# Strassen–Winograd products in 19 of 22 gate and up pairs instead of 12, with the weight sums begun from the first head

## The chip, the cores and the metric

The kernel runs on one core of a Trainium2 chip. The metric is the device time of one execution in microseconds; several executions were timed, and their median counts. The core has a TensorE (PE) that multiplies, with a loader for its weights (PEld), a VectorE (DVE), a ScalarE (ACT), a GpSimd (POOL) and a SyncE (SP), which run their own instruction streams in order. DMA transfers are issued from the streams of SP, ACT and POOL; in the profile SP's transfers are queue q1 and POOL's queue q0.

## The reference, cut to what matters

One residual block on 512 tokens of width 1024: two token mixers side by side (a gated delta rule with 8 heads, and a convolution of 31 taps), a projection, then a SwiGLU channel mixer of hidden width 2816, then a norm. All in float32.

```python
h = rmsnorm(x, norm1_w[l])
proj = h @ w_in[l]
...                                   # 8 heads of the gated delta rule -> out_a; convolution -> out_b
...                                   # gates, w_out and the residual give x; then the channel mixer:
h = rmsnorm(x, norm2_w[l])
gate, up = jnp.split(h @ ffn_w_gate_up[l], 2, axis=-1)
x = x + (jax.nn.silu(gate) * up) @ ffn_w_down[l]
...
return rmsnorm(x, norm_f_w)
```

2816 hidden columns are 22 tiles of 128. For each there is a gate tile and an up tile, 1024 x 128 weights each; this is a "pair" below.

## The kernel before, in words

Every float32 product is made of three: an operand is split into a rounded high part and the rest (`whi`, `wlo` for weights, `hh`, `hl` for the normed tokens), and `split3` issues high by high, high by low and low by high. All weights come through `unit()`: a load of up to 512 KB into `raw` on SP's queue, a copy to `whi` on ACT (L111), a subtraction to `wlo` on DVE (L112). Buffers rotate in a pool, and a load waits only for its buffer.

The program has three stages. **Phase 1** (the page's 0 to about 420 us) walks over 8 heads. A queue of generators yields one set of products after another, and `count` counts its steps; conv, decay and solve work of the heads is hung between them, so each engine's stream mixes several heads. Of a head's work POOL does a power of the key norms (`ss`, L464), a scaling (`Un`, L474), small copies (`cp`, `cc`, L481 to L486), then a solve of 15 dependent steps (`ytm`, `y`, L502 and L504, which need `U`, brought by eight DMAs), and the masks of the decays (`DT`, L444). ACT takes `DT` at L449, the scaled keys at L512 (`Vp`), the solution `y` at L557. **The middle** (to about 603 us) is the output projections, gates and the second norm. **The channel mixer** computes gate and up, 22 pairs, then the down product, itself in Strassen–Winograd form.

A gate and up pair can be computed in two ways. The plain way (`for f in range(F0)`) is 2 weight tiles by 8 contraction tiles by 3 products = 48 products of 512 columns. The other, `pair(f)`, takes gate and up as the two rows, the contraction halves and the token halves as the rest of a 2 by 2 by 2 block product, and needs 7 block products for 8: 7 x 4 x 3 = 84 products of 256 columns. It needs sums of token blocks (`T1` to `T4`, made once by the list `todo`, each item a DVE or ACT step over 128x1024) and four sums of weight blocks for every pair, `s1` to `s4`, 256 KB each. After its 84 products DVE combines the blocks (`cu`, `cv`, `cw`, `fm`).

The sums of weights are made in DRAM, without an engine: `feed_one()` takes the next item of the list `feed`, copies one weight block to the sum's tile (SP's queue, L192), and two items later POOL issues a DMA that adds the other block onto it (L196). `s2` adds `s1`, and `s4` adds `s2`, so these wait for the sum before. In phase 1 nothing is fed until `count` reaches 335; from there `fill()`, called in every `unit()`, feeds one item in two of three calls, later in each, and also makes sums of the down weights on POOL (`dsums_add`, L172, `wst`, `wsh`). `issue_after` sets an instruction behind another in its engine's stream; a scheduler sets the rest.

`pair(f)` uses four PSUM banks for its block results, from two pools: `bank()` is one of the five of `psw`, `bank2()` one of the three of `psm`. Even and odd pairs take four and one of the five. The down product that follows takes four banks of `psw` (`p1`, `p5`).

Of the kernel before, what the change touches and what calls it, by code (L numbers as in the profile page):

```python
# [20 lines left out]
FF = 22  # L21
# [11 lines left out]
def block_kernel(ctx, tc, a):  # L33
# [51 lines left out]
    def marked(b, kind="drain"):  # L85
        mark[b.ins.engine, kind] = b.ins
        return b

    @contextmanager
    def behind(only=None):  # L90
        with ExitStack() as st:
            for i in list(mark.values()):
                if only is None or i.engine == only:
                    st.enter_context(tc.issue_after(i))
            yield

    loads, start_feed, gps_ = [], [False], []

    last = [None]

    def unit(ap, pool=None):

        aps = ap if isinstance(ap, tuple) else (ap,)
        n = T * len(aps) if isinstance(ap, tuple) else 1024
        raw, hi, lo = ((pool or wp).tile([P, n if pool else 1024], t, name=x)[:, 0:n]
                       for t, x in ((F32, "raw"), (F32R, "whi"), (F32R, "wlo")))
        for i, p in enumerate(aps):
            loads.append(nc.sync.dma_start(raw[:, i * T:(i + 1) * T] if len(aps) > 1 else raw, p))
        if start_feed[0]:
            fill()  # L110
        marked(S.activation(hi, raw, AF.Copy), "unit")  # L111
        marked(V.tensor_tensor(out=lo, in0=raw, in1=hi.bitcast(F32), op=ALU.subtract), "unit")  # L112
        return hi, lo
# [31 lines left out]

    FK, F0 = FF // 2, 10
    sums = {n: dram.tile([FF - F0, P, T], F32, name=n, bufs=1) for n in ("s1", "s2", "s3", "s4")}
    gu = {n: a["wgu"][r * FF + F0:(r + 1) * FF][:, :, c * T:(c + 1) * T]  # L150
          for n, r, c in (("A11", 0, 0), ("A12", 0, 1), ("A21", 1, 0), ("A22", 1, 1))}
# [16 lines left out]
    def dsums_add(k, r, cs=slice(0, T)):  # L168
        b11, b12, b21, b22 = (r[:, i, :] for i in range(4))
        with tc.issue_after(last[0].ins):  # L170
            for o, x, y in ((b22, b12, b22), (b12, b11, b12), (b11, b22, b11), (b21, b11, b21)):
                G.tensor_tensor(out=o, in0=x, in1=y, op=ALU.add)  # L172
        nc.gpsimd.dma_start(wsum[k][:, :, cs], r)

    def half_load():
        k, cs = halves.pop(0)
        if len(gps_) == 1:
            r = gps_[0].tile([P, 16, NT, 16], F32, name="U", bufs=2)
            r = r.rearrange("p k n c -> p (k n c)").rearrange("p (i c) -> p i c", i=4)
        else:  # L180
            r = gps_[1].tile([P, 4, 256], F32, name="wsh", bufs=1)
        with tc.issue_after(loads[-1].ins):
            dsums_load(k, r, nc.sync, cs)
        taken.append((k, r, cs))

    def feed_one(n=1):

        for _ in range(n):
            if feed:
                w, p, m, other = feed.pop(0)  # L190
                with tc.issue_after(loads[-1].ins):
                    nc.sync.dma_start(sums[w][p], gu[m][p])  # L192
                begun.append((sums[w][p], other[p]))
        while len(begun) > (2 if feed else 0):
            with tc.issue_after((fed[-1] if fed else last[0]).ins):
                fed.append(nc.gpsimd.dma_start(*begun.pop(0), accum_op=ALU.add, max_dma_last_dim=2048))  # L196
# [3 lines left out]
    def fill():  # L200

        units[0] += 1
        if units[0] % 3 != 2 or not gps_:
            feed_one()
        if taken and units[0] % 3 != 2 and not norming[0]:
            dsums_add(*taken.pop(0))
        if halves and gps_ and units[0] > 3 and not taken and not norming[0] and (units[0] % 2 == 0 if len(gps_) == 1 else units[0] % 3 == 0):
            half_load()
# [528 lines left out]
    def step():  # L737

        while queue:
            try:  # L740
                next(queue[0])
            except StopIteration:
                queue.pop(0)
                continue
            count[0] += 1
            if count[0] % 8 == 0:
                background()
            return True
        return False
# [15 lines left out]
    def background():  # L765
        prio = tc.cur_priority
        tc.cur_priority = prio + OFF
        while len(convs) < len(cs):
            conv31(len(convs), cs[len(convs)])
            convs.append(1)  # L770
        tc.cur_priority = prio
# [63 lines left out]
    done, ended, dts, convs, count, chains = [], [], [], [], [0], [[0, decays()]]  # L835
# [4 lines left out]
    queue.append(rest)  # L840
    nh = 0
    while step() or chains:
        start_feed[0] = count[0] >= 335
        if nh < H and count[0] >= START - 9 + 32 * nh + sum(OTHERS[:nh]):
            chains.append([0, chain(*done[nh])])
            nh += 1
        for c in list(chains):
            if c[0] <= count[0] or not queue:
                with behind():
                    n = next(c[1], None)  # L850
                if n is None:
                    chains.remove(c)
                else:
                    c[0] = count[0] + n
    background()
    for _, sc, e in ended:
        if not sc:
# [170 lines left out]
    def hidden():  # L1028
        fms.append(fp.tile([P, T], F32, name="fm"))
        return fms[-1]  # L1030
# [38 lines left out]
    def negated():  # L1069
# [4 lines left out]
    todo = [joined(b11, kl, t1), joined(b12, kl, t2), lambda: tt(b11, b11, b12, ALU.subtract),  # L1074
            joined(b22, kh, t2), lambda: tt(b12, b22, b12, ALU.subtract),
            lambda: tt(b22, b22, b11, ALU.add), joined(b21, kh, t1),
            lambda: tt(b21, b22, b21, ALU.subtract),
            lambda: xsplit(*T4, b21), negated, lambda: xsplit(*T3, b12)]
# [3 lines left out]
    def some_operands(f):  # L1082
        if not ff:
            fxs.close()
            ff.append(ctx.enter_context(tc.tile_pool(name="ff", bufs=FK)))
        for _ in range(3 if f < F0 else 2):
            if len(made) <= f:
                operands(len(made))
                made.append(1)

    def next_todo():
        if todo:
            with behind():
                todo.pop(0)()

    for f in range(F0):
        start_feed[0] = f > 0
        dsums_to(f)
        if f > 1:
            pg = psm.tile([P, T], F32, name="mm")  # L1100
            col_tile(pg, a["wgu"][f], hhk, hlk)
        else:
            pg = first[2 * f][0]
            k_loop(*first[2 * f], slice(2 * P, T))
        sg = fq.tile([P, T], F32, name="cw", bufs=2)
        S.activation(sg, pg, AF.Silu)
        if f:
            next_todo()
            pu = psm.tile([P, T], F32, name="mm")
            col_tile(pu, a["wgu"][FF + f], hhk, hlk)  # L1110
        else:
            pu = first[1][0]
            k_loop(*first[1], slice(2 * P, T))
        tt(hidden(), pu, sg, ALU.mult)
        if f:
            next_todo()
        if f > 6:
            some_operands(f)

    def hprod(ps, w, i, x):  # L1120

# [4 lines left out]
    bank = lambda: psw.tile([P, T], F32, name="w")  # L1126
    bank2 = lambda: psm.tile([P, T], F32, name="mm")

    def pair(f):

        z = [bank() for _ in range(4)] if f % 2 == 0 else [bank(), bank2(), bank2(), bank2()]
        s = lambda n: sums[n][f - F0]
        w = unit(a["wgu"][f])
        w46 = unit((a["wgu"][FF + f][:, T:], s("s2")))
        hprod(z[0][:, t1], w, 0, B11)
        hprod(z[1][:, t1], w, 1, B21)
        hprod(z[2][:, t1], w46, 0, T4)
        w37 = unit((s("s4"), s("s3")))
        hprod(z[0][:, t2], w46, 1, T2)
        cw = fq.tile([P, T], F32, name="cw", bufs=2)  # L1140
        S.copy(out=cw[:, t1], in_=z[0][:, t1])
        u = fq.tile([P, TH], F32, name="cu")
        tt(u, cw[:, t1], z[0][:, t2], ALU.add)
        hprod(z[1][:, t2], w37, 0, B22)
        w5 = unit((s("s1"),))
        hprod(z[3][:, t1], w37, 1, T3)
        v = fq.tile([P, TH], F32, name="cv2")
        tt(v, u, z[3][:, t1], ALU.add)
        if f == F0:
            xsplit(*T1, b11)  # L1150
        hprod(z[2][:, t2], w5, 0, T1)
        tt(cw[:, t2], u, z[2][:, t2], ALU.add)
        fm = hidden()
        tt(fm.rearrange("p (i t) -> p i t", i=2), z[2].rearrange("p (i t) -> p i t", i=2),
           v.rearrange("p (a t) -> p a t", a=1).broadcast_to([P, 2, TH]), ALU.add)
        tt(cw, cw, z[1], ALU.add)
        S.activation(cw, cw, AF.Silu)
        V.scalar_tensor_tensor(out=fm, in0=fm, scalar=-1.0, in1=cw, op0=ALU.mult, op1=ALU.mult)
# [230 lines left out]
```

## Time and profile before

| | |
|---|---|
| time, median of 3 runs (lowest to highest) | 941.8 us (941.11 to 942.73) |
| the profiled execution | 943.44 us, span 941.7 us |
| granted TensorE clock | 0.997 |
| busy share of the span | PE 98%, PEld 83%, DVE 79%, ACT 59%, POOL 36% |
| q1 (SP's transfers) | 144.89 MB, 44.9% of the 16 DMA engines' span |
| q0 (POOL's transfers) | 28.90 MB, 13.3% |
| accumulating transfers (L196) | 48, 256 KB each |

A row of the chain of waits has a start, a length and what filled it. A group's row has its busy time, the mean in ns, and after a second bar the idle time of its engine just before it, with what ended it. A row of the timeline has start, length, engine, line and operation; the bracket is the idle time before it and what released it.

### The profile page before, as it was taken

What the parts mean: (1) busy time and instruction counts of PE and PEld (TensorE: products, weight loads), DVE (VectorE), ACT (ScalarE), POOL (GpSimd) and SP (SyncE); (2) the same over time, 40 slices, a digit from 0 to 9 for tenths busy, and PEclk for the clock granted to TensorE, in tenths of its full rate; (3) what the DMA queues carried; (4) which work ended last, traced back from release to release, by engine and by line L of the source; (5) the groups of instructions that cost most, each with busy time, mean ns of one, the idle gap of its engine ahead of it and who ended that gap; (6) DMA issues with size and microseconds to landing.
All of it is one profiled execution on the core that took longest, in us unless ns stands there. A gap on an engine that the chain in (4) does not pass through costs nothing.

```text
span 941.7 us, 14545 instructions
## 1 busy us (share of the span) xinstructions
PE 925.4 (98%) x4952; PEld 785.3 (83%) x4952; DVE 740.8 (79%) x1157; ACT 558.0 (59%) x1278; POOL 336.8 (36%) x541
## 2 busy tenths in 40 slices
PE   9999999999999999999999999999999999999996
PEld 6777788878888888888888888988889999988885
DVE  4889898989989899999587643676536877888896
ACT  6696977888778796643555323324324445466545
POOL 0134345253353437544055341245531111133042
PEclk9999999999999999999999999999999999999999
DMA  9333413223123246989898983699797564577654
GB/s 322 113 114 118 131 68 103 86 85 108 73 77 103 93 136 159 335 263 268 284 286 279 285 236 127 205 292 288 257 257 213 184 197 168 186 236 255 213 181 148
DMA packets 78187, 177.39 MB, mean 188 GB/s; under 512 B 10080, under 2 KB 19472, under 8 KB 77088
## 3 DMA queue, kind: packets, MB, share of 16 engines
q1 hardware_dynamic: 66528, 144.89, 44.9%
q0 software_dynamic: 10288, 28.90, 13.3%
q10 hardware_dynamic: 1296, 2.67, 0.7%
q8 instruction: 39, 0.64, 0.3%
q14 instruction: 36, 0.29, 0.1%
HBM read 156.22 MB, written 45.37 MB: 214 GB/s over the span
## 4 chain that ended last, share of the span: by engine, by line
PE 82%; ACT 7%; DVE 3%; issue 1%; POOL 1%; DMA 1%; POOLq 0%; ACTq 0%; DVEq 0%; SPq 0%
PE mm L121 55%; PE w L121 20%; PE b L526 2%; DVE wlo L112 1%; ACT whi L111 1%; PE g L435 1%; PE g L470 1%; PE st L639 1%; PE st L630 1%; PE st L638 1%; PE st L624 1%; PE st L625 0%; ACT Un L473 0%; DVE xs L964 0%; PE b L435 0%
## 5 line engine op out<-in xcount | busy, mean ns | idle before, releaser
L111 ACT ACTIVATE whi<-raw 128x1024 fp32r<-128x1024 f32 (+1 forms) x191 | 196.4, 1030 | 242.6 <-PE mm L121 158.0
L112 DVE TENSOR_TENSOR wlo<-raw,whi 128x1024 fp32r<-128x1024 f32 (+1 forms) x191 | 239.6, 1256 | 86.1 <-ACT whi L111 84.8
L121 PE MATMUL mm<-hh,whi 128*128 128x512 f32 (+1 forms) x688 | 269.7, 392 | 1.2 <-ACT whi L111 0.8
L121 PE MATMUL mm<-hh,wlo 128*128 128x512 f32 (+1 forms) x688 | 264.2, 385 | 0.8 <-DVE wlo L112 0.8
L121 PE MATMUL mm<-hl,whi 128*128 128x512 f32 (+1 forms) x688 | 263.0, 382 | 0.0
L693 DVE SCALAR_TENSOR_TENSOR cps<-c,c31w,cps 128x512 f32<-128x512 f32 x224 | 167.9, 749 | 3.8
L121 PEld LDWEIGHTS mm<-hh,wlo 128*128 128x128 f32 x688 | 130.0, 189 | 25.0 <-DVE wlo L112 1.3
L121 PEld LDWEIGHTS mm<-hh,whi 128*128 128x128 f32 x688 | 130.3, 189 | 22.9 <-ACT whi L111 1.7
L121 PEld LDWEIGHTS mm<-hl,whi 128*128 128x128 f32 x688 | 130.3, 189 | 20.9
L1022 POOL TENSOR_TENSOR fm<-fm 128x256 f32<-128x256 f32 x33 | 28.1, 852 | 117.7 <-DVE s L1022 93.2
L422 DVE SCALAR_TENSOR_TENSOR acc<-mm,c4w,acc 128x511 f32<-128x511 f32 (+2 forms) x72 | 53.0, 740 | 4.3 <-ACT acc L419 4.1
L502 POOL TENSOR_TENSOR ytm<-U,y 128x60 f32<-128x60 f32 (+14 forms) x120 | 36.7, 306 | 51.0 <-DMA U<-sc 42.2
L121 PE MATMUL mm<-yh,whi 128*128 128x512 f32 x128 | 50.6, 396 | 0.0
L121 PE MATMUL mm<-yh,wlo 128*128 128x512 f32 x128 | 49.8, 389 | 0.0
L121 PE MATMUL mm<-yl,whi 128*128 128x512 f32 x128 | 49.8, 389 | 0.0
L121 PE MATMUL w<-hh,wlo 128*128 128x256 f32 x168 | 47.7, 284 | 0.3 <-DVE wlo L112 0.3
L121 PE MATMUL w<-hh,whi 128*128 128x256 f32 x168 | 47.6, 284 | 0.0
L121 PE MATMUL w<-hl,whi 128*128 128x256 f32 x168 | 47.5, 283 | 0.0
L196 POOL DMA_DIRECT2D s<-in_wgu_dram x24 | 22.7, 962 | 64.0 <-DMA s<-in_wgu_dram 64.0
L121 PE MATMUL w<-wlo,fh 128*128 128x512 f32 (+1 forms) x115 | 44.3, 385 | 0.2 <-DVE wlo L112 0.2
L121 PE MATMUL w<-whi,fl 128*128 128x512 f32 (+1 forms) x115 | 44.2, 385 | 0.0
L121 PE MATMUL w<-whi,fh 128*128 128x512 f32 (+1 forms) x115 | 44.2, 385 | 0.0
(346 smaller groups left out, 1937.5 us busy)
## 6 DMA issues: line engine op xcount, KB each, us to landing
raw<-in_win_dram SPq DMA_DIRECT2D x61, 512.0 KB, 3.2
raw<-in_wgu_dram SPq DMA_DIRECT2D x32, 512.0 KB, 3.2
s<-in_wgu_dram SPq DMA_DIRECT2D x48, 256.0 KB, 5.3
raw<-s SPq DMA_DIRECT2D x48, 256.0 KB, 3.6
raw<-wsum SPq DMA_DIRECT2D x44, 256.0 KB, 3.6
raw<-in_wdn_dram SPq DMA_DIRECT2D x33, 256.0 KB, 3.2
s<-in_wgu_dram POOLq DMA_DIRECT2D x24, 256.0 KB, 6.8
s<-s POOLq DMA_DIRECT2D x24, 256.0 KB, 7.2
```

Source lines behind the costliest of these rows:

```text
L111: marked(S.activation(hi, raw, AF.Copy), "unit")
L112: marked(V.tensor_tensor(out=lo, in0=raw, in1=hi.bitcast(F32), op=ALU.subtract), "unit")
L121: marked(PE.matmul(ps, l, r, start=first and i == 0, stop=last and i == 2))
L196: fed.append(nc.gpsimd.dma_start(*begun.pop(0), accum_op=ALU.add, max_dma_last_dim=2048))
L422: marked(V.scalar_tensor_tensor(out=acc[:, s:], in0=ps[:, :T - s], scalar=c4w[:, j, k:k + 1], in1=acc[:, s:], op0=ALU.mult, op1=ALU.add))
L435: PE.transpose(ps[:, n, :], src[:, n, :], ident)
L470: PE.matmul(ps[:, n, :], kT[:, n, :], kT[:, n, :], start=True, stop=True)
L502: G.tensor_tensor(out=tm[:, :, 0:w], in0=U[:, k, :, k + 1:], in1=y[:, :, k:k + 1].broadcast_to([P, NT, w]), op=ALU.mult)
L526: PE.matmul(ps[:, q, 0:w], stationary[:, q, :], moving[:, q, :], start=True, stop=True)
L624: PE.matmul(ps[:, 0, :], kT[:, n, :], Sp, start=True, stop=True)
L693: V.scalar_tensor_tensor(out=acc if k < 30 else cv[i], in0=c[:, k:k + T], scalar=c31w[:, i, k:k + 1], in1=acc if k > 1 else cv[i], op0=ALU ...
L1022: return eng.tensor_tensor(out=out, in0=in0, in1=in1, op=op)
```

## The change

`F0` goes from 10 to 3, so pairs 3 to 21 (19) use 7 block products and pairs 0 to 2 the plain way; the list `feed` grows from 48 to 76 items. A flag `ahead` is set from step 64 of phase 1: every `unit()` then feeds one item, until `fill()` takes over at step 335 as before. The items of `todo` are done two at a time, in the three plain pairs and in the first calls of `pair`. The late operands of the down product (`some_operands`) come only from the loop over pairs, two per call. The choice of the PSUM banks counts from `F0`, so the last pair (21) now takes four of `psw`, where it took one.

```diff
+        elif ahead[0]:
+            feed_one()
...
-    FK, F0 = FF // 2, 10
+    FK, F0 = FF // 2, 3
...
     while step() or chains:
+        ahead[0] = count[0] >= 64
         start_feed[0] = count[0] >= 335
...
+    ahead[0] = False
...
-        for _ in range(3 if f < F0 else 2):
+        for _ in range(2):
...
     def next_todo():
-        if todo:
+        for _ in todo[:2]:
             with behind():
                 todo.pop(0)()
...
-        if f:
-            next_todo()
-        if f > 6:
-            some_operands(f)
+        next_todo()
...
     def pair(f):
-        z = [bank() for _ in range(4)] if f % 2 == 0 else [bank(), bank2(), bank2(), bank2()]
+        z = [bank() for _ in range(4)] if (f - F0) % 2 == 0 else [bank(), bank2(), bank2(), bank2()]
         s = lambda n: sums[n][f - F0]
         w = unit(a["wgu"][f])
+        next_todo()
```

Lines behind the second edit stand two lower in the changed kernel (L196 is L198, L464 is L466). Three places in the streams show what moves. The first is POOL in phase 1, between the end of head 1's solve (`y`) and the start of head 2's. Before:

```order
L504 TENSOR_TENSOR y_1056<-y_1056,ytm_1100 128x4 [waits Pool_49]
L464 TENSOR_TENSOR ss_1452<-ss_1452,root4_85 128x4 [waits DVE_49]
L474 TENSOR_TENSOR Un_1476<-Un_1476,DT_991 128x512 [waits Activation_49]
L481 COPY cp_1482<-Un_1476 32x128 [waits Pool_49]
L481 COPY cp_1482<-Un_1476 32x128 x3
L484 TENSOR_SCALAR cc_1483<-cp_1482,cst_76 128x64 [waits Pool_49]
```

The same place in the changed kernel:

```order
L506 TENSOR_TENSOR y_1056<-y_1056,ytm_1100 128x4 [waits Pool_49]
L198 DMA s1_125<-in_wgu_dram 128x512
L198 DMA s3_127<-in_wgu_dram 128x512
L198 DMA s2_126<-s1_125 128x512 [waits DMASW2_49]
L198 DMA s1_125<-in_wgu_dram 128x512
L198 DMA s4_128<-s2_126 128x512 [waits DMASW4_49]
L466 TENSOR_TENSOR ss_1460<-ss_1460,root4_85 128x4 [waits DVE_49]
L198 DMA s3_127<-in_wgu_dram 128x512
L198 DMA s2_126<-s1_125 128x512 [waits DMASW5_49,DMASW0_49]
L198 DMA s1_125<-in_wgu_dram 128x512 [waits DMAHW2_49,DMASW1_49]
L476 TENSOR_TENSOR Un_1484<-Un_1484,DT_991 128x512 [waits Activation_49]
```

Five accumulating DMAs stand ahead of the norms' power (`ss`), eight ahead of `Un`, and two of the five wait for the accumulate before them to land.

The second is SP behind the second norm's store (`ysp`), where the channel mixer's loads are issued. Before:

```order
L962 DMA ysp<-A 128x1024
L192 DMA s_126<-in_wgu_dram 128x512
L108 DMA raw<-in_wgu_dram 128x1024
L192 DMA s_125<-in_wgu_dram 128x512
L108 DMA raw<-in_wgu_dram 128x1024
L192 DMA s_128<-in_wgu_dram 128x512
L108 DMA raw<-in_wgu_dram 128x1024
```

After, from the fourth unit behind the store on:

```order
L194 DMA s_126<-in_wgu_dram 128x512
L108 DMA raw<-in_wgu_dram 128x512
L108 DMA raw<-s_126 128x512
L194 DMA s_125<-in_wgu_dram 128x512
L108 DMA raw<-s_128 128x512
L108 DMA raw<-s_127 128x512
L194 DMA s_128<-in_wgu_dram 128x512
L108 DMA raw<-s_125 128x512
L194 DMA s_127<-in_wgu_dram 128x512
L108 DMA raw<-in_wgu_dram 128x1024
```

In both a copy follows every unit. Before, 20 copies follow the store and lie beside plain pairs, two units to a pair; now 17 do, and 13 of them lie beside pairs 3 to 6, four units to a pair.

The third is PE at the end of the last pair, where the down product begins. Before:

```order
L121 MATMUL mm_8747<-hh_92,wlo_8835 128x256
L121 MATMUL w_8889<-whi_8894,fh_7101 128x512 [waits Activation_49]
L121 MATMUL w_8889<-whi_8894,fl_7102 128x512
L121 MATMUL w_8889<-wlo_8895,fh_7101 128x512 [waits DVE_49]
L121 MATMUL w_8890<-whi_8894,fh_7101 128x512
L121 MATMUL w_8890<-whi_8894,fl_7102 128x512
L121 MATMUL w_8890<-wlo_8895,fh_7101 128x512
L121 MATMUL w_8891<-whi_8894,fh_7101 128x512 [waits PE_49]
```

After:

```order
L123 MATMUL w_9223<-hh_92,wlo_9311 128x256
L123 MATMUL w_9365<-whi_9370,fh_6939 128x512 [waits Activation_49]
L123 MATMUL w_9365<-whi_9370,fl_6940 128x512
L123 MATMUL w_9365<-wlo_9371,fh_6939 128x512 [waits DVE_49]
L123 MATMUL w_9366<-whi_9370,fh_6939 128x512 [waits DVE_49]
L123 MATMUL w_9366<-whi_9370,fl_6940 128x512
L123 MATMUL w_9366<-wlo_9371,fh_6939 128x512
L123 MATMUL w_9367<-whi_9370,fh_6939 128x512 [waits DVE_49]
```

The second and third banks (`w_9366`, `w_9367`) are ones that the last pair's combination on DVE still reads.

More of the change, by code (lines that the diff above doesn't have):

```diff
@@ L95, in behind @@
             yield
[L97 removed]
+    loads, start_feed, ahead, gps_ = [], [False], [False], []
     last = [None]
```

## The prediction

> **What bounds the kernel now.** I read first the page's engine shares, then the windows by stage, then the chain of waits, then PE's waits, and last the streams of the engines that the change loads. The windows (PE, PEld, DVE, ACT, POOL busy, granted clock, DMA share, GB/s):
>
> ```profile
> 60.00:420.00 360.00, 354.02 (x1860) 293.27 (x1859) 327.14 (x613) 279.07 (x856) 165.29 (x359) 1.00 0.39 125
> 616.00:708.00 92.00, 92.00 (x408) 76.20 (x407) 51.94 (x44) 28.90 (x40) 43.04 (x40) 1.00 0.90 278
> 646.00:656.00 10.00, 10.00 (x46) 8.29 (x45) 4.59 (x5) 4.51 (x5) 1.71 (x3) 1.00 1.00 312
> 708.00:829.00 121.00, 121.00 (x1009) 120.98 (x1009) 92.92 (x139) 59.47 (x84) 16.98 (x22) 1.00 0.60 190
> 740.00:750.00 10.00, 10.00 (x86) 10.00 (x85) 7.94 (x13) 5.01 (x7) 1.54 (x2) 1.00 0.58 185
> ```
>
> PE is busy without a gap where gate and up are computed, in the plain pairs (616 to 708) and the 7-product pairs (708 to 829) alike. So a product less there is time less, as long as nothing else comes late. The chain of waits, in order of time, gives the price of both kinds:
>
> ```profile
> 615.49 92.51 PE mm L121 x408
> 708.00 11.51 PE w L121 x96
> 719.51 2.88 PE mm L121 x24
> 722.39 1.44 PE w L121 x12
> 723.83 4.32 PE mm L121 x36
> 728.15 11.52 PE w L121 x96
> ...
> 808.79 11.52 PE w L121 x96
> 820.31 2.88 PE mm L121 x24
> ```
>
> 408 products of 512 columns took 92.51 us, 0.2268 each; a plain pair is 48, 10.886 us. From 708.00 to 728.15 two 7-product pairs run: 96 + 24 + 12 + 36 = 168 products of 256 columns in 20.15 us, 0.1199 each; a pair is 84, 10.08 us. The gain is 0.81 us a pair, 7.4% and not an eighth, since half the columns cost 53% of the time.
>
> **The products.** Seven pairs (3 to 9) change kind: 7 x 0.81 = **-5.64 us**. The three plain pairs left stay as they are.
>
> **The bank at the end.** The last pair now takes four `psw` banks, so the down product's third bank is the one `cw` reads last. DVE's rows there before:
>
> ```profile
> 829.71 0.41 DVE L1022 TENSOR_TENSOR cw<-cu,mm 128x256 f32<-128x256 f32 x1
> 830.04 0.68 DVE L1022 TENSOR_TENSOR fm<-mm,cv 128x512 f32<-128x512 f32 x1
> 830.64 0.68 DVE L1022 TENSOR_TENSOR cw<-cw,mm 128x512 f32<-128x512 f32 x1
> 828.78 0.40 PE L121 MATMUL w<-whi,fh 128*128 128x512 f32 x1
> ```
>
> The down product begins at 828.78, wants its third bank six products later, 828.78 + 6 x 0.2268 = 830.14, and the last reader ends at 831.32. PE is in order, so it stands for **+1.2 us**. Ends: 0, if DVE's `cw` comes ahead of `fm` there; 2.4, if the subtraction for the next weights, which stands behind these three, is then late too. I take 1.2, which two rows of this place give.
>
> **Phase 1.** 28 more copies and 28 more accumulates; all items ahead of step 335 are new there, so POOL's part is not 28 but about 35 instructions between the heads. One accumulate's price, and how long until the next may follow:
>
> ```profile
> L196 POOL DMA_DIRECT2D s<-in_wgu_dram x24 | 22.7, 962 | 64.0 <-DMA s<-in_wgu_dram 64.0
> L196 POOL DMA_DIRECT2D s<-s x24 | 21.6, 901 | 42.0 <-DMA s<-s 28.2 <-DMA s<-in_wgu_dram 13.7 <-issue 0.2
> 366.85 0.81 POOL L196 DMA_DIRECT2D s<-s  x1 [0.62 <-DMA s<-in_wgu_dram]
> 372.55 0.81 POOL L196 DMA_DIRECT2D s<-s  x1 [1.09 <-DMA s<-s]
> ```
>
> About 0.9 us of POOL each, some 32 us over phase 1, in which POOL is busy 165 of 360. Dearer is the wait: 372.55 - 366.85 = 5.7 us from one accumulate to the one that needs it. Head 2 is the worst place:
>
> ```profile
> 133.79 1.03 POOL L464 TENSOR_TENSOR ss<-ss,root 128x4 f32<-128x4 f32 x1 [8.47 <-DVE ss L462]
> 141.45 0.35 ACT L512 ACTIVATE Vp<-g,ss 128x128 f32<-128x128 f32 x1
> 160.11 0.21 POOL L504 TENSOR_TENSOR y<-y,ytm 128x4 f32<-128x4 f32 x1
> 161.28 1.29 POOL L444 TENSOR_TENSOR DT<-DT,cst 128x512 f32<-128x512 f32 x1
> 162.61 0.40 ACT L449 ACTIVATE DT<-DT,sm 128x128 f32<-128x128 f32 x1 [2.95 <-POOL DT L444]
> 184.43 0.34 ACT L557 ACTIVATE YY<-y,cst 128x64 f32<-128x64 f32 x1
> ```
>
> POOL is free from 125.32 (133.79 - 8.47). Five accumulates with two waits: 125.32 + 2 x 5.7 + 0.8 = 137.5, so `ss` ends near 138.5, 3.7 us later than its 134.8, and ACT wants it at 141.45: hidden. Six more stand ahead of the solve; with 0.9 each and a wait or two I put the end of `y` about 10 us later, near 170, against ACT's `YY` at 184.43: hidden. Then `DT` comes near 174 instead of 162.6. ACT's stream has also moved there: its `DT` step now stands behind a weight copy, the key's activation and three more steps, about 168.5 by the lengths of those in the trace; ACT waits some 5.5 us where it waited 2.95. Behind it in ACT's stream stand the reads of PSUM for the next convolutions; a bank of PE is 24 products x 0.2268 = 5.4 us, so PE has one bank's cover, and ACT idles 29.7 us for PE in this stretch, in which it can catch up:
>
> ```profile
> ACT whi L111 <- PE mm L121: 29.7, 15, 4.1
> ```
>
> I take **+0.7 us**. Ends: -1 (PE's few microseconds of waits in phase 1 fall otherwise in the new order) and +6 (two such waits, each a few microseconds past the cover). The copies on SP's queue are 28 x 256 KB over some 260 us at a DMA share of 0.39; the raw loads there have time in hand, so nothing for them.
>
> **Transfers beside pairs 3 to 6.** This is the disputed term. Before, the copies lay beside plain pairs; their load was 0.90 of the engines over 92 us and PE never stood, not even at 1.00 (646 to 656). Now 13 copies lie beside four pairs, one a unit. A pair's loads are 3 x 512 + 256 KB = 1.84 MB, its copies 1.05 MB: 2.9 MB in 10.08 us on q1, 286 GB/s; the `wst` loads of 1 MB and their stores, one of each in two pairs, add 100 GB/s on q0, a third of that, without the accumulates. The windows have 278 to 312 GB/s at 0.90 to 1.00. So for pairs 3 to 6 the demand is some 20% above what those windows moved: over 30 us about 6 us of transfers fall behind. What a pair has in hand, and the transfers' sizes and landings:
>
> ```profile
> 817.39 1.06 ACT L111 ACTIVATE whi<-raw 128x1024 fp32r<-128x1024 f32 x1 [1.56 <-PE w L121]
> 818.83 1.06 ACT L111 ACTIVATE whi<-raw 128x1024 fp32r<-128x1024 f32 x1 [0.38 <-PE w L121]
> 818.49 1.23 DVE L112 TENSOR_TENSOR wlo<-raw,whi 128x1024 fp32r<-128x1024 f32 x1 [0.60 <-ACT whi L111]
> raw<-in_wgu_dram SPq DMA_DIRECT2D x32, 512.0 KB, 3.2
> s<-in_wgu_dram SPq DMA_DIRECT2D x48, 256.0 KB, 5.3
> wst<-in_wdn_dram POOLq DMA_DIRECT2D x4, 1024.0 KB, 8.1
> ```
>
> ACT's copies wait for PE to free a buffer, not for the load. The `wlo` of 818.49 ends at 819.72, and PE needs that unit 36 products into the pair that starts at 818.87 (808.79 + 84 x 0.12): counted with the first product of its high part, 24 after, 821.75. So 2.0 us in hand behind ACT and DVE, and about 1 us ahead of them, since a load must also wait for its buffer: landings may grow from 3.2 to about 6 us before PE stands. Of 6 us behind, some 3 to 4 are covered, and 2 would reach PE. I take **+1.5 us**: ends 0 (646 to 656, no PE wait at full load) and +6 (all the backlog).
>
> **POOL's additions beside DVE.** Three of the four `wst` bursts now lie beside 7-product pairs, where DVE is busy 7.94 of 10 us:
>
> ```profile
> 655.74 6.62 POOL L172 TENSOR_TENSOR wst<-wst 128x512 f32<-128x512 f32 x4 [6.05 <-DMA wst<-in_wdn_dram]
> 617.94 2.31 DVE L112 TENSOR_TENSOR wlo<-raw,whi 128x1024 fp32r<-128x1024 f32 x1
> 643.62 1.23 DVE L112 TENSOR_TENSOR wlo<-raw,whi 128x1024 fp32r<-128x1024 f32 x1
> ```
>
> A subtraction takes 2.31 us beside an addition and 1.23 alone. Such two-input steps are about 0.6 of DVE's work in a pair, so in 6.62 us of additions DVE falls 5.3 x 1.53 - 6.62 = 1.5 us behind; there are 2.0 us in hand: **+0.3 us** for the three, from 0 to 3.
>
> The Trainium skill (SBUF — State Buffer, "Who interferes with whom") says that a DVE step with two SBUF inputs and a GpSimd step that reads SBUF exclude each other for the whole instruction. The 2.31 against 1.23 agrees with a wait, of 1.08 us and not of an addition's whole 1.66 (6.62 / 4); by the rule at its worst the term would be the port rival's below.
>
> **The rest.** `todo` has the same 11 steps, now two at a time: by their lengths (1.22 us each) the operands are ready near 630, before pair 3 begins at 615.49 + 72 x 0.2268 = 631.8 us; nothing, though the margin is 1 to 2 us. The late operands are spread one or two per pair; ACT is busy 5.01 of 10 us. The 59 sums fed before the channel mixer are early for pair 3. Nothing each.
>
> Sum: -5.64 + 1.2 + 0.7 + 1.5 + 0.3 = -1.9 to -2.3 (the margins overlap, so I round to **-2.2**). The profiled execution took 943.44 us, span 941.7, 1.6 above the median of 941.8; the sum against it gives 941.2, against the median **939.6 us**.
>
> **The rivals.**
> (a) All is hidden but the bank, or not even that: -5.64 + 0 to 1.2, 936.2 to 938. For it: PE did not stand at DMA share 1.00. Against it: the doubled units per time.
> (b) The transfers eat the gain: the term is 4 to 6 instead of 1.5, 941 to 943.7. For it: copies and raw loads share one queue, in order, so each load stands behind a 256 KB copy that took 5.3 us at the median. The Trainium skill (DMA: Bandwidth & Descriptors, "Queues, rings and completion order") has the engines take turns between queues packet by packet, which would give POOL's transfers an equal turn against the loads while both have work; no row of before splits the two, and the rule speaks for this rival.
> (c) Slower: POOL's stream in phase 1. If accumulates land in 8 us rather than 5.7, beside 15 dependent steps, `DT` comes at 180, not 174, ACT stands for some 11 us and PE runs out of free banks after 5.4: +6 at each of the two late `DT`, so -5.64 + 1.5 + 2 x 5 = +6: 945 to 949. It decides from an ACT wait of about 5.4 us on. Against it: 24 us in hand at `YY`, and only those places.
> (d) The port: each of three `wlo` in a burst waits out a whole addition of 1.66 us (6.62 / 4), 5 us late, 3 past what is in hand, in two or three bursts: -5.64 + 1.2 + 0.7 + 6 to 9, 944 to 947. For it: DVE is busier there than before. Against it: 2.31 us, not 2.9, is the longest `wlo` of before.
>
> **How the numbers follow.** This kernel's runs spread by 0.17%, so a change of under 0.2% (1.9 us) counts as none; faster means below 939.9, slower above 943.7. Forecast, 938.3 to 941.0: 0.42, of which 0.26 below 939.9. (a) 0.18, faster. (b) 0.22, within. (c) 0.12 and (d) 0.06, slower. Faster 0.44, same 0.38, slower 0.18. The range, 936.8 to 945.3, leaves out the lower third of (a) and most of (c), and the forecast's own range is the one named above.
>
> **What would show it.** Right: PE rows of 7-product pairs from 631.8 on in the chain at 10.08 us each; a gap of about 1.2 us on PE behind six down products, ended by DVE; PE waits of 1 to 2 us on `whi` or `wlo` in the first four such pairs, none later; `DT` on ACT waiting 4 to 6 us near 170 with PE's phase 1 ending within 1 us of before. Wrong: the output projections' start later by over 3 us, for (c); over 3 us of waits in pairs 3 to 6 ended by a DMA, for (b), or by `wlo` during `wst`, for (d); none of all these, for (a).

## The result: slower, and the profile after

The changed kernel takes 965.55 us (median of 4 runs, 964.2 to 965.84) against 942.1 before (median of 4); the ratio is 1.0247, interval 1.0229 to 1.0265. The profiled run took 964.2 us with a span of 962.4, so 20.7 us more than the span before. The chain of waits divides it. These are its rows at the start of the channel mixer, at pair 3, where the first unbroken 7-product pair comes back, and at the last pair (start, length, what):

```profile
612.02 11.52 PE w L123 x96
623.54 16.35 PE mm L123 x72
639.88 10.09 PE w L123 x84
...
719.32 11.52 PE w L123 x96
...
840.28 40.82 PE w L123 x219
```

The row of 96 small products that opens the channel mixer stood at 603.97 before and is at 612.02 now: **8.05 us are lost ahead of the channel mixer**. That is one execution's figure: in five experiments below whose phase 1 is edited no further, the row stands 4.6 to 9.75 us late, so it moves by several microseconds. The three plain pairs take what they took (72 products in 16.35). Pair 3 begins at 639.88, right behind them. The pairs from 719.32 on run without a wait, two in 20.16 us, to the last at 840.28; 719.32 is then pair 9, and pairs 3 to 8 took 79.44 us instead of 6 x 10.08 = 60.48: **19.0 us are lost there**. From the last row, 40.82 - 84 x 0.12 = 30.74 us go to the down product's first 135 products, against 30.63 before. With the products' -5.64 and -0.7 behind the pairs, 8.05 + 19.0 - 5.64 - 0.7 = 20.7.

The windows of phase 1 where it is lost, and of pairs 3 to 8 (PE, PEld, DVE, ACT, POOL busy, granted clock, DMA share, GB/s). The first row is the kernel before, the others are the changed kernel:

```profile
140.00:200.00 60.00, 59.49 (x324) 49.02 (x323) 52.97 (x107) 51.59 (x164) 26.36 (x64) 1.00 0.27 90
140.00:200.00 60.00, 54.16 (x272) 44.74 (x271) 45.06 (x92) 40.45 (x135) 34.84 (x64) 0.91 0.71 164
144.00:146.00 2.00, 2.00 (x7) 1.51 (x6) 1.26 (x2) 1.94 (x7) 1.89 (x3) 0.50 1.12 199
182.00:184.00 2.00, 0.00 (x0) 0.00 (x0) 2.00 (x5) 2.00 (x7) 1.35 (x1) 1.00 0.00 0
186.00:188.00 2.00, 1.76 (x8) 1.76 (x9) 1.93 (x4) 1.96 (x10) 1.91 (x2) 0.50 0.77 256
188.00:190.00 2.00, 2.00 (x10) 2.00 (x10) 1.34 (x4) 1.92 (x7) 1.73 (x5) 0.50 0.53 201
640.00:708.00 68.00, 58.40 (x443) 56.42 (x442) 40.57 (x53) 23.57 (x34) 31.52 (x28) 0.94 0.97 304
711.00:714.00 3.00, 3.00 (x16) 3.00 (x16) 2.26 (x4) 2.10 (x3) 0.81 (x1) 0.50 0.76 195
```

Two things are to be seen. In 140 to 200 and in 640 to 708 PE is idle for 5.8 and 9.6 us. And behind the idle stretches the granted clock is 0.50 for some microseconds, though PE is busy again: 144 to 146, 186 to 190, 711 to 714. The loss is idle time and half speed together; the busy time hides the second part. Of the 79.4 us of pairs 3 to 8 PE is idle for 11.4, at a mean clock of 0.91; the other 7.6 us of the 19.0 are mostly slower running. At 140 the changed kernel was ahead (ACT's `Un` of head 2 at 133.86 against 135.67 before), so 140 to 200 lost somewhat more than the 8.05. In 640 to 708 the transfers are at 0.97 of the 16 engines for 68 us.

Who waited in phase 1, by the streams of POOL, ACT, DVE and PE:

```profile
127.33 1.85 POOL L198 DMA_DIRECT2D s<-in_wgu_dram  x2
133.60 0.81 POOL L198 DMA_DIRECT2D s<-s  x1 [4.43 <-DMA s<-in_wgu_dram]
139.26 0.81 POOL L198 DMA_DIRECT2D s<-s  x1 [4.01 <-DMA s<-s]
139.81 1.33 POOL L466 TENSOR_TENSOR ss<-ss,root 128x4 f32<-128x4 f32 x1
141.17 0.37 ACT L514 ACTIVATE Vp<-g,ss 128x128 f32<-128x128 f32 x1 [1.44 <-POOL ss L466]
142.48 0.49 PE L640 MATMUL st<-w,kd 128*128 128x128 f32 x2 [1.54 <-ACT R L637]
172.39 0.21 POOL L506 TENSOR_TENSOR y<-y,ytm 128x4 f32<-128x4 f32 x1
173.95 1.92 POOL L446 TENSOR_TENSOR DT<-DT,cst 128x512 f32<-128x512 f32 x1
175.90 1.28 ACT L451 ACTIVATE DT<-DT,sm 128x128 f32<-128x128 f32 x4 [4.26 <-POOL DT L446]
180.43 0.75 DVE L424 SCALAR_TENSOR_TENSOR acc<-mm,c4w,acc 128x511 f32<-128x511 f32 x1 [4.98 <-ACT acc L421]
184.56 0.47 PE L123 MATMUL mm<-hh,whi 128*128 128x512 f32 x1 [3.07 <-DVE ss L468]
```

The bracket at the end of each row is the wait. POOL waits 4.43 and 4.01 us for one accumulate and then the next, so `ss`, `y` and `DT` of head 2 come late. Behind `ss` ACT waits 1.44 us and PE 1.54. Behind `DT` ACT waits 4.26 us, DVE 4.98 for ACT's copy of a convolution, and PE 3.07 for DVE. The profile names DVE's small step `ss` as the releaser of PE; that PE waits for a PSUM bank is an inference, from DVE's reading of a bank (`acc<-mm`, L424) up to 184.42, just ahead of PE's 184.56.

Who waited beside the pairs, 636 to 722 us, from the waits view (total, times, longest):

```profile
ACT whi L113 <- DMA raw<-s: 32.2, 13, 7.7
DVE wlo L114 <- ACT whi L113: 29.2, 14, 6.9
PE mm L123 <- ACT whi L113: 4.8, 1, 4.8
PE w L123 <- DVE wlo L114: 3.0, 5, 0.9
```

The weights land late, and ACT, DVE and PE wait behind one another.

### The profile page after: what moved, and what is told of

Read it like the earlier page. It is cut to its first block, busy times and chain, and to the rows that moved or that the text cites. A ratio compares the mean times of both kernels' runs of the same rounds, so it can differ in the third digit from the quotient of the medians.

```text
span 962.4 us, 15283 instructions
## 1 busy us (share of the span) xinstructions
PE 930.9 (97%) x5204; PEld 800.3 (83%) x5204; DVE 761.7 (79%) x1206; ACT 568.6 (59%) x1297; POOL 367.0 (38%) x569
## 4 chain that ended last, share of the span: by engine, by line
PE 68%; DMA 8%; ACT 6%; DVE 6%; POOL 4%; issue 2%; SPq 1%; POOLq 0%; ACTq 0%; DVEq 0%
PE mm L123 40%; PE w L123 22%; DMA raw<-s 4%; DVE wlo L114 2%; PE b L528 1%; DMA U<-sc 1%; POOL ytm L504 1%; ACT whi L113 1%; DVE cps L695 1%; POOL y L506 1%; PE st L641 1%; DMA s<-in_wgu_dram 1%; PE g L437 1%; POOL s L198 1%; DMA s<-s 1%
## 5 line engine op out<-in xcount | busy, mean ns | idle before, releaser
L123 PE MATMUL mm<-hh,whi 128*128 128x512 f32 (+1 forms) x612 | 236.3, 387 | 4.2 <-DVE ss L468 3.1
L123 PE MATMUL mm<-hh,wlo 128*128 128x512 f32 (+1 forms) x612 | 231.4, 378 | 0.2 <-DVE wlo L114 0.2
L123 PE MATMUL mm<-hl,whi 128*128 128x512 f32 (+1 forms) x612 | 230.2, 376 | 0.0
L123 PE MATMUL w<-hh,wlo 128*128 128x256 f32 x244 | 71.1, 291 | 3.0 <-DVE wlo L114 3.0
L123 PE MATMUL w<-hh,whi 128*128 128x256 f32 x244 | 70.8, 290 | 2.9 <-ACT whi L113 2.9
L198 POOL DMA_DIRECT2D s<-s x38 | 33.9, 892 | 103.7 <-DMA s<-in_wgu_dram 83.3
L123 PE MATMUL w<-hl,whi 128*128 128x256 f32 x244 | 70.5, 289 | 0.0
L424 DVE SCALAR_TENSOR_TENSOR acc<-mm,c4w,acc 128x511 f32<-128x511 f32 (+2 forms) x72 | 53.1, 740 | 8.5 <-ACT acc L421 8.3
L123 PEld LDWEIGHTS w<-hh,wlo 128*128 128x128 f32 x244 | 48.3, 198 | 4.1 <-DVE wlo L114 4.0
L123 PEld LDWEIGHTS w<-hh,whi 128*128 128x128 f32 x244 | 48.2, 198 | 3.4 <-ACT whi L113 3.3
L123 PEld LDWEIGHTS w<-hl,whi 128*128 128x128 f32 x244 | 48.2, 198 | 0.0
```

Source lines behind the costliest of these rows:

```text
L123: marked(PE.matmul(ps, l, r, start=first and i == 0, stop=last and i == 2))
L424: marked(V.scalar_tensor_tensor(out=acc[:, s:], in0=ps[:, :T - s], scalar=c4w[:, j, k:k + 1], in1=acc[:, s:], op0=ALU.mult, op1=ALU.add))
```

## The experiments

Theory P: the accumulates in POOL's stream lose the 8 us of phase 1. Theory T: the transfers beside the pairs lose the 19. Rival S for the second: POOL's additions of the down weights' sums. "Lost in the pairs" is worked out for each run as above, from the chain's first and last pair rows; "start" is the row of 96 products that opens the channel mixer, 603.97 before.

**Early feed with F0 = 10.** Edit:

```diff
-    FK, F0 = FF // 2, 3
+    FK, F0 = FF // 2, 10
```

> F0 back to 10 (12 pairs of 7 products), everything else as in the changed kernel: the early feed from step 64 stays, and the 48 sums are all made before the channel mixer. Theory P (the 8 us lost before the channel mixer are the price of the early feed, whatever F0 is): the channel mixer begins 7 to 9 us later than before, no PE wait in the pairs, 949 to 951 us. Rival (they come from the scheduler's other order for F0 = 3): begins within 1.5 us of before, 941 to 943.5 us.

950.42 us, ratio 1.0083 (1.0063 to 1.0103). The start is at 611.34, 7.4 us late, and nothing is lost in the pairs. The loss of phase 1 belongs to the early feed and not to F0 = 3.

**Copies early, accumulates late.** Edit in `feed_one`:

```diff
-        while len(begun) > (2 if feed else 0):
+        for _ in range(2 if start_feed[0] else 0):
+            if len(begun) <= (2 if feed else 0):
+                break
```

> The copies still begin at step 64, but the accumulating DMAs on POOL only at step 335, then up to two per unit. Theory P (the accumulates stand in POOL's in-order stream ahead of the heads' work): the channel mixer begins within 1.5 us of before; the pairs lose about as much as in the changed kernel (19 us): 956 to 960 us. Rival D (the copies' load on the DMA engines delays the heads' small transfers): the start stays 6 to 9 us late, 963 to 967 us.

994.7 us, ratio 1.0553 (1.0526 to 1.058): far off as a time, and still the run that settles phase 1. Its windows:

```profile
140.00:200.00 60.00, 59.49 (x316) 48.94 (x315) 53.49 (x107) 49.36 (x159) 27.69 (x69) 1.00 0.40 128
340.00:500.00 160.00, 130.10 (x605) 107.28 (x603) 104.37 (x176) 68.31 (x183) 87.35 (x122) 0.90 0.94 237
```

With the copies alone, 140 to 200 has 59.49 us of PE at full clock, as before the change (59.49), and nothing is lost up to 340. So the copies alone do no harm there, and the accumulates do: P. How they do it, the trace shows for `ss`, which stands behind POOL's waits of 4.43 and 4.01 us; no run separates their place in POOL's stream from what they load on the DMA engines (0.71 of them in 140 to 200 in the changed kernel, 0.40 here). The some 35 accumulates that were put off then stood in POOL's stream from 340 on, ahead of the last heads' work and the down weights' sums, and PE lost 30 us of 160 with a clock of 0.90. Neither theory had reckoned with that; both times given were wrong.

**No copies and accumulates beside the pairs.** Pairs 17 to 21 read pair 16's sums:

```diff
-        s = lambda n: sums[n][f - F0]
+        s = lambda n: sums[n][min(f - F0, 13)]
...
-                   "s4": ("A12", sums["s2"])}[w[0]]) for w in feed if w[1] < FF - F0]
+                   "s4": ("A12", sums["s2"])}[w[0]]) for w in feed if w[1] < 14]
```

> Pairs 17 to 21 read the sums of pair 16, so 56 sums are made instead of 76 and no copy and no accumulate is left beside the pairs (the output differs there). Theory T (beside pairs 3 to 8 the transfers ask for more than the DMA engines move): without 13 copies and some 17 accumulates the demand is about 280 GB/s and the 19 us go but for 0 to 3: 946 to 950 us. Rival W (the loads, stores and additions of the down weights' sums cost most of it): 5 to 8 us go, 957 to 961 us.

951.19 us, ratio 1.012 (1.0063 to 1.0178): 14.4 us under the changed kernel. In the profile 7.1 us are still lost in the pairs (the changed kernel: 19.0). That is between the theories.

**No sums of the down weights beside the pairs.** Loads, additions and stores of `wst` go, the copies stay:

```diff
-    rest = [(k, cs) for k, cs in halves]
+    kept, rest = halves[0][0], []
...
-    wt = lambda k, i: wsum[k][:, {1: 1, 2: 0, 3: 3, 4: 2}[i], :]
+    wt = lambda k, i: wsum[k % kept][:, {1: 1, 2: 0, 3: 3, 4: 2}[i], :]
```

> The sums of the down weights that are made beside the pairs (loads, stores and additions of wst) are left out, and the down product reads the earlier sums in their place (the output differs there); the feed stays. Theory T (bytes): 4 MB in and 4 MB out fewer over 70 us, q0's share falls by more than half, 10 to 16 of the 19 us go, 950 to 956 us. Rival Q (each raw load waits behind a copy on SP's in-order queue): 0 to 4 us go, 961 to 966 us.

950.6 us, ratio 1.0083 (1.005 to 1.0116): 15.0 us under, 4.7 lost in the pairs. The profiled execution, 946.39 us, was the shortest of the four, so the 4.7 may be on the low side. Rival Q (the order of SP's queue) falls as the main cause: all the copies are still there. Either half of the load, taken away, brings back most; neither alone explains it. This run took away two things, POOL's additions and the 1 MB transfers; the next two runs part them.

**Without POOL's additions.** As the run without copies beside the pairs, and in `dsums_add` (`ff_on` is filled just ahead of the channel mixer):

```diff
-            for o, x, y in ((b22, b12, b22), (b12, b11, b12), (b11, b22, b11), (b21, b11, b21)):
+            for o, x, y in () if ff_on else ((b22, b12, b22), (b12, b11, b12), (b11, b22, b11), (b21, b11, b21)):
```

> As the run without copies beside the pairs, and POOL's additions on the down weights' tiles beside the pairs are left out too, their 1 MB loads and stores stay (the output differs there). Theory T (the 7 us that this run still lost beside pairs 3 to 8 come from the 1 MB transfers, which lengthen the raw loads' landings): 5 to 8 us are still lost, 948 to 952 us. Rival S (they come from POOL's additions, which make DVE's subtractions 2.3 us long): 0 to 2.5 us are lost, 943.5 to 947 us.

944.67 us, ratio 1.0032 (1.002 to 1.0044), 6.5 us under the run with the additions. Chain, from pair 3 on:

```profile
641.59 11.51 PE w L123 x96
653.10 2.88 PE mm L123 x24
...
661.74 11.55 PE w L123 x96
```

Two pairs in 20.15 us: nothing is lost in the pairs, with the 1 MB loads and stores still there. What the additions did is in DVE's rows of the run that had them, 660.3 to 666.9 us being one burst:

```profile
662.01 2.04 DVE L114 TENSOR_TENSOR wlo<-raw,whi 128x1024 fp32r<-128x1024 f32 x1 [1.95 <-ACT whi L113]
663.97 1.77 DVE L1160 SCALAR_TENSOR_TENSOR fm<-fm,cw 128x512 f32<-128x512 f32 x1
665.67 1.78 DVE L114 TENSOR_TENSOR wlo<-raw,whi 128x512 fp32r<-128x512 f32 x1
667.37 0.41 DVE L1023 TENSOR_TENSOR fl<-fm,fh 128x256 fp32r<-128x256 f32 x1
```

Each of the first three rows, two-input steps, is longer by about as much whatever its size: 0.8 us more on 1.22, 1.1 more on 0.68 twice. That is 3 us in one burst. Rival S is right for the 7 us of that run.

**Copies, without the additions.** The changed kernel with that last edit alone:

> The changed kernel with all its copies, accumulates and 1 MB transfers beside the pairs, only POOL's additions on the down weights' tiles are left out there (the output differs). Theory S (the additions, by DVE's longer subtractions, are the larger part of the 19 us): 10 to 14 us go, 951 to 955 us. Theory T (the transfers are): 4 to 8 us go, 957 to 962 us.

959.07 us, ratio 1.0192 (1.0165 to 1.022), 6.5 us under, 13.1 lost in the pairs. So of 19.0 us in the profiles, the additions are 5.9 with the copies there (19.0 - 13.1) and 7.1 without; the copies and accumulates are 11.9 with the additions (19.0 - 7.1) and 13.1 without, as long as the 1 MB transfers are there (4.7 without them). T and S both hold; T is the larger part. The landings of the weights in 640 to 705 us (256 KB loads, median us to landing), in the order changed kernel, without additions, without copies, without both:

```profile
raw<-s SPq DMA_DIRECT2D x20, 256.0 KB, 6.8
raw<-s SPq DMA_DIRECT2D x20, 256.0 KB, 7.3
raw<-s SPq DMA_DIRECT2D x24, 256.0 KB, 4.7
raw<-s SPq DMA_DIRECT2D x24, 256.0 KB, 3.7
```

How the two queues share the engines (packets, MB, share of the 16 engines), first in the changed kernel from 640 to 705, then before from 640 to 705, beside plain pairs, and last q1 before beside the 7-product pairs (708 to 829), where it had hardly anything but the raw loads:

```profile
q1 hardware_dynamic: 5524, 11.38, 49.1%
q0 software_dynamic: 2249, 8.31, 47.5%
q0 software_dynamic: 2376, 8.27, 49.5%
q1 hardware_dynamic: 3666, 9.04, 38.5%
q1 hardware_dynamic: 10497, 21.75, 53.9%
```

The raw loads of 7-product pairs alone took 53.9% without a PE wait. In the changed kernel q1 got 49.1% for these loads and the copies, beside 47.5% for q0; in the run without the additions it was 48.5% and 47.3%, again a loss. Before, q0 was as busy, but q1 took only 38.5% beside plain pairs. So a likely reason is that q1 fell short of its need once q0 was as busy as it; no run changed only the sharing, so this is not shown.

**Spread transfers.** A copy in two units beside the pairs, the down weights' sums in eight halves (`made` is empty up to the first 7-product pair):

```diff
-        if units[0] % 3 != 2 or not gps_:
+        if units[0] % 3 != 2 if gps_ else units[0] % 2 or len(made) == 0:
...
-            if rest and rest[0][0] == k:
-                rest.pop(0)
-                cs = slice(0, T)
```

> As the changed kernel, but beside the pairs a copy follows every second unit instead of every unit, and the down weights' sums come in eight half tiles (512 KB), one in two pairs, instead of four whole ones (1 MB). Same work, spread over twice the time. Theory T (what hurts is how much is asked for at a time: 1 MB loads, copies and accumulates ahead of raw loads): 12 to 18 of the 19 us go, 948 to 954 us, with the 8 us of phase 1 left. Rival V (the total is what counts, and spreading only moves it to later pairs): 0 to 6 us go, 960 to 966 us.

959.42 us, ratio 1.0179 (1.0146 to 1.0212): only 6 us go. 14.1 us are lost, over ten pairs instead of six; the transfers' share is 0.89 from 637 to 752. Rival V was nearer: at this rate spreading moves the loss.

**Spread transfers and a later start.** As the last, and:

```diff
-        ahead[0] = count[0] >= 64
+        ahead[0] = count[0] >= 156
```

> As the run with the spread transfers, and the early feed starts at step 156 instead of 64, behind head 2's solve. Theory P: phase 1 loses 0 to 2 us instead of 8; 28 copies are left for the pairs instead of 17, at one in two units they reach to pair 15 or so. With theory T for the pairs: 936.5 to 941 us. Rival (a later head loses the 8 us in the place of head 2, since its accumulates stand as much in the way): 946 to 952 us.

962.71 us, ratio 1.019 (1.0147 to 1.0233). The start was at 608.59, 4.6 us late, lost in 200 to 260 now: part of it went over to a later head. More copies were left for the pairs, and 23.0 us were lost there. Both expectations failed.

**F0 = 7 with the later start.** Nothing is spread:

```diff
-    FK, F0 = FF // 2, 3
+    FK, F0 = FF // 2, 7
...
-        ahead[0] = count[0] >= 64
+        ahead[0] = count[0] >= 156
```

> F0 = 7 (15 pairs of 7 products), early feed from step 156, transfers beside the pairs as in the changed kernel. Copies and the down weights' sums lie beside plain pairs then, as in the kernel before. Theory T: no waits in the pairs, 3 x 0.81 = 2.4 us less than before plus 0 to 2 us of phase 1: 939.5 to 942 us. Rival (phase 1 loses as much with the later start): 946 to 949 us.

943.9 us, ratio 1.0012 (0.9993 to 1.0031), no difference. The start is at 606.21, 2.2 us late, and nothing is lost in 14 pairs (677.60 to 818.96). The three pairs' 2.4 us and the 2.2 of phase 1 cancel.

**Another order of sums.** F0 = 10, the feed from step 64, each sum four items behind what it adds and accumulates four items behind their copies:

```diff
-    feed = [("s1", 0)] + [w for p in range(FF - F0) for w in (("s3", p), ("s2", p), ("s1", p + 1), ("s4", p))]
+    feed = [("s1", 0), ("s1", 1), ("s3", 0), ("s2", 0)]
+    feed += [w for p in range(FF - F0) for w in (("s1", p + 2), ("s3", p + 1), ("s2", p + 1), ("s4", p))]
...
-        while len(begun) > (2 if feed else 0):
+        while len(begun) > (4 if feed else 0):
```

> F0 = 10 with the feed from step 64 (950.4 us, against 942.2 before), but the list of sums in another order, so that a sum stands four items behind the one it adds, not two or three, and an accumulate follows its copy four items later instead of two. As many accumulates on POOL, fewer waits between them. Theory P1 (the waits of one accumulate for the other hold POOL up, not the 0.9 us of each): 4 to 7 of the 8 us go, 943 to 946 us. Rival P2 (the number of instructions does): 0 to 2 us go, 948 to 950.5 us.

949.01 us, ratio 1.0077 (1.0062 to 1.0093): no clear difference from 1.0083 (1.0063 to 1.0103), and the start, 611.48, is as late as 611.34. P1's 4 to 7 us didn't go. But the order didn't take the waits away: one of 5.6 us stood ahead of head 2's `ss` in this run too, PE was idle once for 4.1 us, and 140 to 200 still has a clock of 0.94. So the run leaves open whether the waits or the number of accumulates count for more.

**The same order with F0 = 6.** The last edit, and:

```diff
-    FK, F0 = FF // 2, 3
+    FK, F0 = FF // 2, 6
```

> The same order of sums with F0 = 6 (16 pairs of 7 products). All but five copies are made before the channel mixer, and three of the four bursts of additions lie beside plain pairs. By the products 4 x 0.81 = 3.2 us less than the run with F0 = 10 and this order; theory T and S (copies and additions beside 7-product pairs are what costs): nothing lost in the pairs, so 3 us under that run, 939.5 to 943 us. Rival (the plain pairs no longer hold all of it): 1 us under that run, or above it.

944.11 us, ratio 1.0025 (1.0014 to 1.0036). The start is 4.3 us late, nothing is lost in the pairs, and 3.2 of it come back by the products. It is 4.9 us under the F0 = 10 run, and 6.8 in the two profiled executions (950.74 and 943.91): 3.2 by the products, as expected, and 3.2 by the start, 608.26 against 611.48, which nothing in the edit explains. So much phase 1 moves from build to build or from one execution to the next.

**No early feed, few copies beside the pairs.** F0 = 8 with one copy in three units, and F0 = 7 with one in two (`units[0] % 2` in the place of `units[0] % 3`):

```diff
-    FK, F0 = FF // 2, 3
+    FK, F0 = FF // 2, 8
...
-        if units[0] % 3 != 2 or not gps_:
+        if units[0] % 3 != 2 if gps_ else units[0] % 3 == 0 or not made:
...
-        ahead[0] = count[0] >= 64
+        ahead[0] = False
```

> F0 = 8 (14 pairs of 7 products), no early feed at all, and beside the 7-product pairs one copy in three units; the four bursts of additions stay beside plain pairs. By the products 2 x 0.81 = 1.6 us less than before. Theory T (copies cost nothing there as long as a pair's transfers stay below what the engines move, 1.84 + 0.35 MB of loads and copies and 0.35 of accumulates in 10 us here): nothing lost, phase 1 as before: 939.5 to 941 us against about 941.7. Rival (any copy in a raw load's way costs): 1.5 to 4 us lost, 941.5 to 944.5 us.

> As the run with F0 = 8 and one copy in three units, with F0 = 7 (15 pairs) and one copy in two units, since the sums must be ready sooner: 1.84 + 0.52 MB of loads and copies and 0.52 of accumulates in 10 us. By the products 2.4 us less than before. Theory T: at about 285 GB/s this is at the edge of what the windows moved: 0 to 2 us lost, 939.3 to 941.5 us. Rival (any copy costs): 3 to 5 us lost, 942 to 945 us.

945.17 us (1.0032, 1.0021 to 1.0044) and 953.5 us (1.0111, 1.0095 to 1.0127). Neither time lies in a range given for it, theory T's or the rival's. The windows, first of F0 = 8 in two stretches, then of F0 = 7:

```profile
685.00:720.00 35.00, 32.12 (x249) 31.43 (x248) 19.70 (x30) 14.10 (x20) 4.91 (x6) 0.95 0.95 264
719.00:790.00 71.00, 71.00 (x594) 71.00 (x594) 54.52 (x83) 34.92 (x49) 15.86 (x21) 1.00 0.84 250
720.00:790.00 70.00, 66.26 (x529) 63.88 (x528) 48.91 (x73) 31.37 (x44) 17.47 (x22) 1.00 0.92 259
```

With one copy in three units PE stands for nothing over 71 us at a share of 0.84. With one in two it is idle for 3.7 us of 70 at 0.92, and the loss is larger than that: 529 products stand in these 70 us and 594 in the 71 of the row above, so about 6.5 us are lost, since a product's row lasts 0.28 us where the next one follows after 0.12, and a short wait hides under it. In all its pairs that run lost 14.7 us. So copies cost nothing below a rate, and above it they cost. The F0 = 8 run lost 5.7 us in the pairs, nearly all of it in its first stretch, 0.95, where the copies of the plain pairs, the accumulates behind them and the last store of the down weights' sums ran over into pairs 8 to 10: 2.9 us idle and a clock of 0.95 over 35 us. No version tried beat the kernel before.

## Why the prediction was wrong, point by point

It forecast 939.6 us in a range from 936.8 to 945.3; 965.6 was measured. The terms that it lists add up to -1.9 and not to the -2.2 that it rounds to, which matters little here.

- **The products, -5.64: right.** The undisturbed pairs take 10.08 us in every run. Nothing was lost for the token blocks' sums either: pair 3 begins right behind the plain pairs.
- **The bank at the end, +1.2: wrong, 0.1.** The down product's first 135 products took 30.74 us against 30.63. The step that failed is which bank the third is: it was taken to be the one that `cw` reads last. DVE's last read of that bank and PE's first product in the third and in the fourth bank:

```profile
852.05 0.68 DVE L1026 TENSOR_TENSOR cw<-cw,w 128x512 f32<-128x512 f32 x1
851.58 0.39 PE L123 MATMUL w<-whi,fh 128*128 128x512 f32 x1
852.28 0.47 PE L123 MATMUL w<-whi,fh 128*128 128x512 f32 x1
```

Both begin before that read has ended (852.73), the third 1.39 us behind the first product as before the change. So that bank isn't among those wanted so early.

- **Phase 1, +0.7: 8.05.** The mechanism and the times along POOL were right: `ss` to end at 138.5 (141.1 measured), `y` near 170 (172.6), `DT` near 174 (175.9), ACT to stand 5.5 us (6.0: 1.74 for a transfer of `DT` and 4.26 for POOL). The step that failed is "PE has one bank's cover": PE's bank is freed by DVE (the inference above), whose stream was as late as ACT's (4.98 us), and PE stood 3.07 us. `ss`, called hidden with 3 us to spare, was 1.4 us too late for ACT, and PE stood 1.5 us for that: POOL came free at 127.4 instead of 125.3, and ACT wanted `ss` at 139.7 and not 141.45. The second failed step is one that the sum didn't have: behind each of these stops PE ran at half clock, about 4 us behind the first, 6 behind the second. Rival (c) had this chain and its direction, with 0.12, and a point of decision, 5.4 us of ACT's wait, that the 6.0 in all passed and POOL's 4.26 alone did not. Its own premise, accumulates that land in 8 us and `DT` at 180, didn't come: the two waits were 5.7 us from one accumulate to the next, and `DT` came at 175.9.
- **Transfers beside pairs 3 to 6, +1.5: about 12.** The demand was reckoned 20% above what the engines move, and 6 us as the whole backlog. Three parts of that were wrong. Its own figures, 286 and 100 against 278 to 312 GB/s, make it 24 to 39% and not 20. The accumulates on q0 were left out of the demand, though there are as many as copies. And the backlog doesn't end with the copies: the accumulates still run to 712, so the loss went on to pair 8. The upper bound, "all the backlog, 6", was no bound. Then the clock: 7.6 of the 19.0 us here are not idle time, and the sum had no such part. The end of 0 rested on a window at full load beside a plain pair, where q1 needed less; and rows of before do split the two queues (49.5% and 38.5% above), which rival (b) held not to exist.
- **POOL's additions, +0.3: 6 to 7.** The stretch was taken as a factor of 1.53 from the 128x1024 subtraction. It is about 1 us more for each two-input step that falls into a burst, so the small ones more than double, and a burst costs 3 us and not 1.5. The 2.0 us in hand are also smaller than reckoned, since `raw` comes free only when DVE is done: a late subtraction also delays the next load (ACT's wait for raw in the run without copies: 19.7 us in total, against 6.4 without the additions).
- The Trainium skill (SBUF — State Buffer, "Who interferes with whom") has the second to come wait until the first ends. The near-constant extra of 0.8 to 1.1 us, whatever the step's size, agrees with that and not with a factor. Rival (d), built on such a wait, priced the additions at 6 to 9 us, with a chance of 0.06; its size came true, its step did not, since no step above waited an addition's whole 1.66 us.
- **Half clock.** The Trainium skill (TensorE: Matmul & The Clock Gate, "What's actually happening") states that an idle window of about 3.4 us brings the clock to a half until a busy one has passed. The stop of 3.07 us and the 0.50 of the 6 us behind it come near that. The other stops don't fit a length of 3.4: one of 1.54 us at 141 also brought 0.50 for 4 us, and in the run without copies one of 1.4 us at 675 brought none. So in this kernel 3.4 us is no length below which a stop is safe. The sum had no place for any of this.
- The losses were those of rivals (b), (c) and (d), and each rival was priced as if the others were as in the forecast; all three came at once.

## What to carry to other kernels

Where PE is the bound, price a stop of PE at its length and again some microseconds at half clock, and look for any single stop of over a microsecond. When work is put in an engine's idle time, follow what stands behind it in that stream through every engine to PE, and take as cover the slack of the last one. When transfers are moved, add up all queues at the new place, what follows on them included, against what the fullest undisturbed window with the same work beside it moved: here, beside the 7-product pairs, a share of up to 0.84 of the engines cost nothing over 71 us, 0.92 about a tenth of the time, and 0.97, with the additions, a quarter. A full window beside other work is no measure: beside plain pairs a share of 1.00 cost nothing. And look at each queue's share by itself.

## What the runs showed of the hardware that was not expected

- The granted clock was 0.50 for 4 to 6 us behind stops of 1.5 and 3.1 us in phase 1; one of 1.4 us in the run without copies had no such effect.
- POOL's additions lengthened the two-input steps of DVE that fell beside them by 0.8 to 1.1 us: 0.68 became 1.77.
- With both queues full, SP's and POOL's got about half of the DMA engines each: 49.1% and 47.5%, 48.5% and 47.3%.
- Two loads on the 16 engines that cost little alone (1 MB transfers: 0 us lost; copies and accumulates without them: 4.7) lose 13 us together. Why the copies lose 4.7 us at a share of 0.87 (640 to 700) in that run, and those of the F0 = 8 run none at 0.84, was not taken further; nor was which of the accumulates in phase 1 is the one too many.
